# Blocks 12 to 15 of the first token group by Strassen's scheme too, its weight sums on GpSimd

## The chip, the cores and the metric

The kernel runs on one core of a Trainium2 chip. Such a core has a matrix engine (TensorE, PE in the profile; its weight loads are PEld), a vector engine (VectorE, DVE), an activation engine (ScalarE, ACT), a general one (GpSimd, POOL) and SyncE (SP), which here issues most DMAs. SBUF is the memory on the core with 128 partitions; PSUM holds the results of matmuls in banks. Each engine works through its own queue in order and waits on semaphores for the others.

The metric is the device time of one launch in microseconds (us). Times of several runs are given with their median; a profiled execution is one run more, of which a trace is kept.

## The reference

One layer of a streaming encoder for 2048 prompt tokens and 64 sample tokens: a modulated RMSNorm, one input projection, a pooling mixer beside an mLSTM, an output projection, then a second modulated RMSNorm and a gated MLP with a causal convolution of width 3. The change lies in the MLP:

```python
h2 = rmsnorm(x, g2) * (1 + sc2) + sh2
up = h2 @ w_up                                     # 1024 -> 2 * 2816
upp = jnp.concatenate([conv_buf.astype(up.dtype), up], 1)
conv = b_conv + sum(w_conv[j] * upp[:, j:j + T] for j in range(CONV_W))
a, g = jnp.split(conv, 2, -1)
x = x + gt2 * ((jax.nn.silu(g) * a) @ w_down)      # 2816 -> 1024
```

All is float32. The kernel gets that accuracy from a faster matmul by splitting each operand in a rounded part and a remainder and making three products of them (`PASSES`).

## The kernel before, in words

The MLP takes the 2112 tokens in three groups of 704 (`fgroups`, groups 0, 1 and 2, the loop `for o in fgroups`). The hidden width 2816 is 22 blocks of 128 (`f`). For each block, `Pair.products` makes the a and the g half of the up projection by a scheme of Strassen's kind: seven products (B11, T1, T2, B21, B22, T3 and, one block later, T4) of 12 matmuls with 352 columns each (L1604), which add into three PSUM banks, instead of eight. For the scheme, sums of the tokens' blocks are needed. They are made for the next group ahead of time by the generator `prepare`, one step at a time: it loads rows of x, scales them, makes seven sums for each of four row pairs, rounds each on ScalarE (L798), takes the remainder on DVE (L784) and further differences (L780), and stores both parts (`Bd`, L850, from ScalarE's queue). Its tiles come from four buffers named fscr.

The rest of a block is spread over the two blocks after it: sums and copies out of PSUM (`eg`, `ea`; L1613 on DVE, L1617 on ScalarE), the convolution (L1577 on ScalarE, two taps of eg and ea each on DVE, L1582), silu (L1801), the gate (L1806, or L1809 in a Strassen part) and the split of the result in two parts (`av`: L1884 on ScalarE and L1889 on DVE). The tiles ea and eg have one buffer each. Their first two columns come from a small buffer UC by a copy on GpSimd (L1560), and their last two go back there (L1574).

Blocks are put together in parts (`PARTS`). After the blocks of a part stands its down projection. A plain part runs `down`: for each of the eight output rows, per block, three matmuls of 448 and three of 256 columns (L2212). A part of four blocks can run `quad_down` instead: Strassen's scheme again, over two by two blocks, seven products in place of eight, 168 matmuls of 352 columns (L2073). Such a part is held: its operands (B11 to T4 of the class `Quad`, seven av tiles, made in `step_2` to `step_7`) are prepared while the next blocks start, and `quad_down` runs inside the first block of the next part. Group 1 does that for its blocks 0 to 19 (five quads), group 2 for 0 to 15 (four); group 0 does not, since `paired` asks for g > 0.

Weights come as a stream of units of 512 columns (`stream`, `issue`, `pump`), loaded up to seven ahead on SP's queue into raw or wt buffers. Each is rounded on ScalarE (L427) and its remainder taken on DVE (L430), some units ahead of use (`work_out`). For the down scheme four sums of weights for each pair of output rows are read from `dsum`, a buffer in DRAM. They are made once, in group 0, by the generator `quad_sums`: 20 halves, each one load (L1660), four tensor ops of 128x256 (L1664 to L1670) and one store (L1673), with pauses between.

What stands where is written by hand: from the MLP on, PE, ScalarE, DVE and GpSimd run in program order, and the order of SP's queue is the scheduler's. Side work is put in through lists (`bg`): `tick(i)` runs list i on to its next pause, `drain(i)` runs it to its end at once. `quad_sums` is in list 0, which gets two ticks in each product (14 a block) and some in `down`; `prepare` is in list 1, which gets four ticks a block and the other ticks of `down`. Where `todo` holds steps of the last blocks, `down` takes those instead of a tick. At the last part's down phase, lists 0 and 1 are drained, and list 1 gets the loads of the next group's operands.

## Time and profile before

| | us |
|---|---|
| median of three runs (2169.93 to 2173.72) | 2172.97 |
| the profiled execution, all in all | 2169.81 |
| its span, first instruction to last | 2168.0 |
| group 0 of the MLP, from its first up product on | 787.2 to 1251.6 |
| of it, its four down phases | 853.7, 959.6, 1078.1 and 1203.9, of 41 to 48 each |
| groups 1 and 2 | 1251.6 to the end |

A row of the profile that groups instructions has line, engine, operation, result<-operands, sizes, count, then busy time in us, mean ns of one, and the idle time of the engine before them with what ended it. A row of the timeline has its start in us, the time it covers, the instructions merged in it, and in square brackets idle time before it. A row of a stretch has its length, then the busy time of PE, PEld, DVE, ACT and POOL with counts in brackets, TensorE's granted clock, the DMA engines' busy share and GB/s. Numbers with L are lines of the kernel before; in the changed kernel the same lines stand one further down behind `SUMS`, and eight further behind the last hunk.

### The profile page before, as it was taken

Reading aid. Unit: us, or ns where it says so; the run is one execution under the profiler, and the core shown is the slowest. Engines: PE = TensorE matmul, PEld = TensorE weight load, DVE = VectorE, ACT = ScalarE, POOL = GpSimd, SP = SyncE. Lnnn points to the kernel's source line nnn. Section 1 sums busy time; section 2 is a strip of 40 time slices with the busy share of each in tenths; the row PEclk is TensorE's granted clock in tenths of the full one; section 3 lists DMA queues with packets and bytes.
Section 4 is the critical chain, followed back from the end, with each engine's and each line's share of the span. In section 5 each row is a group of like instructions: output and inputs, shape, how many; then the busy total and the mean of one; then the engine's idle time right before and its main releaser. Section 6 shows DMA issues by size and latency. Waiting matters only on the chain.

```text
span 2168.0 us, 38128 instructions
## 1 busy us (share of the span) xinstructions
PE 2146.5 (99%) x13529; PEld 2040.9 (94%) x13529; DVE 1666.4 (77%) x3107; ACT 1104.1 (51%) x2201; POOL 249.3 (12%) x468
## 2 busy tenths in 40 slices
PE   8999999999999999999999999999999999999998
PEld 7888888888899999999999999999999999999998
DVE  5777678677675878797968668988888797887874
ACT  4554335334333556464736445655656455565554
POOL 0010000001000301010101220100101121111112
PEclk9999999999999999999999999999999999999999
DMA  8987997897788686888968976666666875555542
GB/s 317 330 307 228 321 317 252 282 320 269 246 286 281 229 268 232 293 288 301 353 235 307 319 264 206 226 227 200 219 232 230 277 269 190 171 175 188 173 157 76
DMA packets 302439, 545.28 MB, mean 252 GB/s; under 512 B 25984, under 2 KB 118656, under 8 KB 302248
## 3 DMA queue, kind: packets, MB, share of 16 engines
q1 hardware_dynamic: 291656, 517.64, 70.6%
q10 hardware_dynamic: 10592, 25.20, 3.0%
q8 instruction: 107, 1.75, 0.3%
q14 instruction: 84, 0.69, 0.1%
HBM read 414.65 MB, written 128.08 MB: 250 GB/s over the span
## 4 chain that ended last, share of the span: by engine, by line
PE 60%; DVE 3%; DMA 1%; issue 1%; ACT 1%; POOL 0%; SPq 0%; DVEq 0%; POOLq 0%; ACTq 0%
PE mm L1604 37%; PE mm L2212 11%; PE mm L2073 10%; PE mm L494 2%; DVE wt L430 1%; DVE tg L1582 0%; ACT tg L1577 0%; DMA wt<-dsum 0%; DMA wt<-wsum 0%; DMA fscr<-h2d 0%; DVE ea L1613 0%; DVE eg L1613 0%; DVE x L2042 0%; DVE tg L1809 0%; ACT mm L1652 0%
## 5 line engine op out<-in xcount | busy, mean ns | idle before, releaser
L1604 PE MATMUL mm<-hx,wt 128*128 128x352 f32 x5544 | 887.1, 321 | 0.9 <-DVE wt L430 0.7
L1604 PEld LDWEIGHTS mm<-hx,wt 128*128 128x128 f32 x5544 | 880.5, 188 | 2.2 <-DVE wt L430 1.9
L494 PE MATMUL mm<-hl,wt 128*128 128x512 f32 (+2 forms) x1920 | 385.8, 356 | 0.3 <-DMA wt<-hl_kept 0.3
L427 ACT ACTIVATE wt<-raw 128x512 fp32r<-128x512 f32 (+3 forms) x468 | 275.9, 597 | 191.0 <-PE mm L494 53.4
L430 DVE TENSOR_TENSOR wt<-raw,wt 128x512 fp32r<-128x512 f32 (+3 forms) x468 | 307.3, 663 | 74.8 <-ACT wt L427 73.3
L494 PEld LDWEIGHTS mm<-hl,wt 128*128 128x128 f32 x1920 | 314.7, 188 | 48.1 <-issue 4.4
L2073 PE MATMUL mm<-av,wt 128*128 128x352 f32 x1512 | 248.2, 324 | 2.7 <-DVE ea L1613 1.2
L2073 PEld LDWEIGHTS mm<-av,wt 128*128 128x128 f32 x1512 | 242.3, 188 | 6.2 <-DVE ea L1613 4.0
L2042 DVE SCALAR_TENSOR_TENSOR x<-mm,MOD,x 128x352 f32<-128x352 f32 (+5 forms) x384 | 180.3, 508 | 69.0 <-PE mm L2212 54.1
L2212 PE MATMUL mm<-av,wt 128*128 128x448 f32 (+1 forms) x1440 | 232.2, 322 | 0.0
L2212 PEld LDWEIGHTS mm<-av,wt 128*128 128x128 f32 x1440 | 221.2, 188 | 9.9
L1652 ACT ACTIVATE mm<-mm 128x352 f32<-128x352 f32 x204 | 91.4, 448 | 235.9 <-PE mm L1604 176.6
L494 PE MATMUL mm<-mx,wt 128*128 128x512 f32 (+1 forms) x960 | 182.2, 351 | 1.2 <-DVE scr L266 1.2
L494 PEld LDWEIGHTS mm<-mx,wt 128*128 128x128 f32 x960 | 158.5, 188 | 24.1 <-DVE scr L266 1.1
L1582 DVE SCALAR_TENSOR_TENSOR ta<-ea,V,ta 128x704 f32<-128x704 f32 (+1 forms) x132 | 125.6, 952 | 54.8 <-ACT ta L1577 48.2
L1582 DVE SCALAR_TENSOR_TENSOR tg<-eg,V,tg 128x704 f32<-128x704 f32 (+1 forms) x132 | 125.7, 952 | 50.5 <-ACT tg L1577 48.0
L430 DVE TENSOR_TENSOR wt<-wt 128x512 fp32r<-128x512 f32 x204 | 138.4, 683 | 11.6 <-ACT wt L427 11.6
L427 ACT ACTIVATE wt<-wt 128x512 fp32r<-128x512 f32 x204 | 123.6, 622 | 34.0 <-DMA wt<-wsum 31.0
L1560 POOL COPY ea<-UC 128x2 f32<-128x2 f32 x66 | 32.7, 496 | 510.4 <-DVE ta L1582 429.1
L1801 ACT ACTIVATE tg<-tg 128x704 f32<-128x704 f32 (+1 forms) x66 | 52.4, 794 | 69.3 <-DVE tg L1582 69.3
L1143 PE MATMUL mm<-wt,hl 128*128 128x256 f32 (+1 forms) x576 | 71.2, 284 | 0.0
L1143 PEld LDWEIGHTS mm<-wt,hl 128*128 128x128 f32 x576 | 70.2, 189 | 0.8 <-issue 0.6
(306 smaller groups left out, 2220.2 us busy)
## 6 DMA issues: line engine op xcount, KB each, us to landing
wt<-wsplit SPq DMA_DIRECT2D x132, 512.0 KB, 4.3
raw<-w_up SPq DMA_DIRECT2D x198, 256.0 KB, 4.3
wt<-hl_kept SPq DMA_DIRECT2D x96, 512.0 KB, 6.3
wt<-wsum SPq DMA_DIRECT2D x132, 256.0 KB, 5.2
wsplit<-wt SPq DMA_DIRECT2D x66, 512.0 KB, 5.4
w<-w_up SPq DMA_DIRECT2D x88, 256.0 KB, 4.8
wsum<-w SPq DMA_DIRECT2D x44, 512.0 KB, 6.0
Bd<-fscr ACTq DMA_DIRECT2D x56, 352.0 KB, 4.4
```

The source lines that it names most:

```text
L427: act.activation(u.w[:, 0, :u.n], u.raw[:, :u.n], AF.Copy)
L430: dve.tensor_tensor(out=u.w[:, 1, :u.n], in0=u.raw[:, :u.n], in1=u.w[:, 0, :u.n].bitcast(F32), op=ALU.subtract)
L494: pe.matmul(ps[bi][:, :hi - lo], U[:, a, k % 4 * P:(k % 4 + 1) * P], mv[k][:, b, lo:hi], start=(at == 0 and pi == 0), stop=(k == order[-1] ...
L1143: pe.matmul(ps[ti][:n, :cols], h[4 * kh + k4][:, b, lo:lo + n], U[:, a, k4 % 2 * cols:(k4 % 2 + 1) * cols], start=(kh == 0 and k4 == 0 and ...
L1560: pool.tensor_copy(ext[:, 0:2], UC[:, f, :])
L1582: dve.scalar_tensor_tensor(out=t[:, :E], in0=ext[:, j:j + E], scalar=wc(j, f), in1=t[:, :E], op0=ALU.mult, op1=ALU.add)
L1604: pe.matmul(bk.t[:, :FH], U[:, a, kc * P:(kc + 1) * P], Bo.at(nm, kc, b), start=(first and kc == 0 and pi == 0), stop=(kc == 3 and pi == 2 ...
L1652: act.activation(to.t[:, :FH], bk.t[:, :FH], AF.Copy)
L1801: act.activation(self.tg[:, :E], self.tg[:, :E], AF.Silu)
L2042: dve.scalar_tensor_tensor(out=x3[n][:, a:b], in0=bk.t[:, a - lo:b - lo], scalar=gt2(n, s), in1=x3[n][:, a:b], op0=ALU.mult, op1=ALU.add)
L2073: pe.matmul(bk.t[:, :FH], U[:, a, c:c + P], quad.put(op, m, b), start=(first and m == 0 and pi == 0), stop=(m == 1 and pi == 2), skip_grou ...
L2212: pe.matmul(bks[i].t[:, :hi - lo], U[:, a, k % 4 * P:(k % 4 + 1) * P], av[k][:, b, lo:hi], start=(k == 0 and (a, b) == PASSES[0]), stop=(k ...
```

## The change

- Group 0's parts become (0, 6), (6, 12), (12, 16), (16, 22), and `paired` no longer asks for g > 0: blocks 12 to 15 of group 0 are a quad, held over into block 16.
- `quad_sums` takes a list of sums to make. The first list has twelve halves (6, 7, 0, 1, 2, 3; the first two are what the new quad reads), the second eight. The four ops of a half go to GpSimd, and a half takes eleven ticks in place of thirteen.
- Ahead of block 12 the first list is drained and list 1 (`prepare`) is put aside; behind `quad_down` it is put back, and the second list starts.
- At the last part's down phase of group 0 only list 1 is drained; list 0 at the end of that phase.

```diff
--- before.py
+++ after.py
@@ -30,13 +30,14 @@
 EB = 1
 AVB = 7
 ENDS = ((0, 448), (448, 704))
-PARTS = (((0, 5), (5, 10), (10, 16), (16, 22)), ((0, 4), (4, 8), (8, 12), (12, 16), (16, 20), (20, 22)),
+PARTS = (((0, 6), (6, 12), (12, 16), (16, 22)), ((0, 4), (4, 8), (8, 12), (12, 16), (16, 20), (20, 22)),
          ((0, 4), (4, 8), (8, 12), (12, 16), (16, 22)))
 NQ, QUADS = 4, 5
+SUMS = ((6, 7, 0, 1, 2, 3), (4, 5, 8, 9))
 
 
 def paired(g, part):
-    return g > 0 and part[1] - part[0] == NQ
+    return part[1] - part[0] == NQ
 EPS = 1e-6
 HD = 128
 NH = 4
@@ -1651,27 +1652,26 @@
 
         act.activation(to.t[:, :FH], bk.t[:, :FH], AF.Copy)
 
-    def quad_sums():
-
-        for d in range(2 * QUADS):
+    def quad_sums(ds):
+
+        for d in ds:
             for c in (0, 256):
                 t = f2.tile([P, 2, FT], F32R, tag="av", name="qs", bufs=AVB)
                 w = t.bitcast(F32).rearrange("p a t -> p (a t)")[:, :1024].rearrange("p (i c) -> p i c", i=4)
                 nc.sync.dma_start(out=w, in_=w_quad[d, :, :, c:c + 256])
-                for _ in range(5):
+                for _ in range(4):
                     yield
                 a11, a12, a21, a22 = (w[:, i] for i in range(4))
-                dve.tensor_tensor(out=a22, in0=a21, in1=a22, op=ALU.add)
-                yield
-                dve.tensor_tensor(out=a21, in0=a11, in1=a21, op=ALU.subtract)
-                yield
-                dve.tensor_tensor(out=a11, in0=a22, in1=a11, op=ALU.subtract)
-                yield
-                dve.tensor_tensor(out=a12, in0=a12, in1=a11, op=ALU.subtract)
+                pool.tensor_tensor(out=a22, in0=a21, in1=a22, op=ALU.add)
+                yield
+                pool.tensor_tensor(out=a21, in0=a11, in1=a21, op=ALU.subtract)
+                yield
+                pool.tensor_tensor(out=a11, in0=a22, in1=a11, op=ALU.subtract)
+                yield
+                pool.tensor_tensor(out=a12, in0=a12, in1=a11, op=ALU.subtract)
                 yield
                 yield
                 nc.sync.dma_start(out=dsum[d, :, :, c:c + 256], in_=w)
-                yield
                 yield
                 yield
 
@@ -2159,6 +2159,9 @@
             ends = o.last and lastp
             av = [None] * nf
             quad = Quad() if paired(o.g, part) else None
+            if quad is not None and o.g == 0:
+                drain(0)
+                aside, bg[1][:] = list(bg[1]), []
             if pi == 0:
                 pair = None
             for f in range(f0, f1_):
@@ -2169,16 +2172,19 @@
                 if held is not None and nf > 2:
                     quad_down(o, held, pair, old)
                     held = None
+                    if o.g == 0:
+                        bg[0].append(quad_sums(SUMS[1]))
+                        bg[1].extend(aside)
             if pi == 0 and o.g > 0:
                 drain(0)
                 x3 += load_x2(o, range(len(x3), KD))
             if not o.last:
                 if pi == 0:
                     if o.g == 0:
-                        bg[0].append(quad_sums())
+                        bg[0].append(quad_sums(SUMS[0]))
                     bg[1].append(prepare(fgroups[o.g + 1], fscr))
                 if lastp:
-                    drain(0, 1)
+                    drain(1) if o.g == 0 else drain(0, 1)
                     if nf == 2:
                         for p in (old, pair):
                             p.d = f1.tile([P, 2, HX], F32R, tag="hx", name="av", bufs=2 * len(BN))
@@ -2276,6 +2282,8 @@
             pair = None
         if not o.last:
             drain(1)
+            if o.g == 0:
+                drain(0)
             if nf == 2:
                 Bn = B[-1]
                 Bn.load(BN[-1])
```

How this moves instructions is shown at three places. ScalarE at the end of group 0, from the last copy of the up products (ea, L1617) to the last silu's followers. Before:

```order
L1617 ACTIVATE ea<-mm 128x352
L427 ACTIVATE wt<-raw 128x512
L1801 ACTIVATE tg<-tg 128x704
L427 ACTIVATE wt<-raw 128x512
L427 ACTIVATE wt<-raw 128x256 x2
L1884 ACTIVATE av<-tg 128x704
```

And in the changed kernel, with the stores of `prepare` (Bd) and its roundings (L799):

```order
L1801 ACTIVATE tg<-tg 128x704
L851 DMA Bd<-fscr 128x704
L799 ACTIVATE fscr<-fscr 128x352
L428 ACTIVATE wt<-raw 128x512
L851 DMA Bd<-fscr 128x704
L799 ACTIVATE fscr<-fscr 128x352
L851 DMA Bd<-fscr 128x704
L799 ACTIVATE fscr<-fscr 128x352
L851 DMA Bd<-fscr 128x704
L799 ACTIVATE fscr<-fscr 128x352
L851 DMA Bd<-fscr 128x704
L428 ACTIVATE wt<-raw 128x256 x2
```

Four roundings and five stores of `prepare` now stand between the silu and the splits of the first 256-column down units; before, none did.

DVE at the same place, from the last taps of g to the sum eg of block 21. Before:

```order
L1582 SCALAR_TENSOR_TENSOR tg<-eg,V,tg 128x704 x2
L430 TENSOR_TENSOR wt<-raw,wt 128x512 x3
L430 TENSOR_TENSOR wt<-raw,wt 128x256
L1613 TENSOR_TENSOR eg<-mm,s_13198 128x352
L1806 TENSOR_TENSOR tg<-ta,tg 128x704
```

In the changed kernel (L785 are remainders, L781 differences of `prepare`):

```order
L1583 SCALAR_TENSOR_TENSOR tg<-eg,V,tg 128x704 x2
L785 TENSOR_TENSOR fscr<-fscr 128x352
L781 TENSOR_TENSOR fscr<-fscr 128x352
L431 TENSOR_TENSOR wt<-raw,wt 128x512 x2
L785 TENSOR_TENSOR fscr<-fscr 128x352
L781 TENSOR_TENSOR fscr<-fscr 128x352 x2
L785 TENSOR_TENSOR fscr<-fscr 128x352 x3
L431 TENSOR_TENSOR wt<-raw,wt 128x512
L431 TENSOR_TENSOR wt<-raw,wt 128x256
L1614 TENSOR_TENSOR eg<-mm,s_13152 128x352
L1806 TENSOR_TENSOR tg<-ta,tg 128x704
```

Eight ops of `prepare` now stand ahead of eg, six of them without other work but the splits between.

GpSimd in blocks 8 and 9 of group 0, from the copy into ea of block 8 on. Before:

```order
L1560 COPY ea<-UC 128x2
L1560 COPY eg<-UC 128x2
L1574 COPY UC<-ea 128x2
L1574 COPY UC<-eg 128x2
L1560 COPY ea<-UC 128x2
```

In the changed kernel (L1665 to L1671 are the four ops of a half of the weight sums):

```order
L1561 COPY ea<-UC 128x2
L1665 TENSOR_TENSOR qs<-qs 128x256
L1667 TENSOR_TENSOR qs<-qs 128x256
L1669 TENSOR_TENSOR qs<-qs 128x256
L1561 COPY eg<-UC 128x2
L1671 TENSOR_TENSOR qs<-qs 128x256
L1575 COPY UC<-ea 128x2
L1575 COPY UC<-eg 128x2
L1561 COPY ea<-UC 128x2
```

Four ops on the weight sums now stand between the copies; before, GpSimd had the copies alone there, and the ops were DVE's.

## The prediction

> **What bounds the kernel now.** I read the page first (busy shares, chain, groups), then the timeline of TensorE for the stretch that the change touches, then DVE block by block, then the rows in which GpSimd and DVE meet.
>
> ```profile
> span 2168.0 us, 38128 instructions
> PE 2146.5 (99%) x13529; PEld 2040.9 (94%) x13529; DVE 1666.4 (77%) x3107; ACT 1104.1 (51%) x2201; POOL 249.3 (12%) x468
> PE 60%; DVE 3%; DMA 1%; issue 1%; ACT 1%; POOL 0%; SPq 0%; DVEq 0%; POOLq 0%; ACTq 0%
> L1604 PE MATMUL mm<-hx,wt 128*128 128x352 f32 x5544 | 887.1, 321 | 0.9 <-DVE wt L430 0.7
> ```
>
> TensorE is busy 99% of the span and leads the chain; the up products (L1604) idle 0.9 us in all. So only fewer matmuls can shorten the kernel, and any late operand lengthens it one for one. How near the operands are to late is read from the opening group by blocks. The next rows are stretches of one block each (blocks 12 to 15 with sums and preparation beside them, then 18 to 21 with sums in three of the four and no preparation): length, then busy time of PE, PEld, DVE, ACT and POOL with counts in brackets.
>
> ```profile
> 1024.88:1038.18 13.30, 13.30 (x87) 13.30 (x85) 12.60 (x22) 9.77 (x18) 2.58 (x4) 1.00 0.96 342
> 1038.18:1051.48 13.30, 13.30 (x87) 13.30 (x85) 12.44 (x21) 8.98 (x16) 2.75 (x4) 1.00 1.05 392
> 1051.48:1064.80 13.32, 13.32 (x87) 13.28 (x85) 13.18 (x22) 10.43 (x19) 2.56 (x4) 1.00 1.00 325
> 1064.80:1078.10 13.30, 13.30 (x87) 13.30 (x85) 12.82 (x23) 9.67 (x19) 2.13 (x4) 1.00 1.01 353
> ...
> 1150.67:1163.97 13.30, 13.30 (x86) 13.30 (x85) 12.10 (x20) 8.95 (x16) 2.29 (x4) 1.00 0.90 321
> 1163.97:1177.27 13.30, 13.30 (x87) 13.30 (x85) 12.01 (x20) 9.16 (x16) 2.30 (x4) 1.00 0.96 334
> 1177.27:1190.57 13.30, 13.30 (x87) 13.30 (x85) 12.01 (x20) 9.39 (x17) 2.30 (x4) 1.00 0.89 318
> 1190.57:1203.87 13.30, 13.30 (x86) 13.30 (x85) 10.66 (x16) 9.08 (x18) 2.29 (x4) 1.00 0.94 316
> ```
>
> With sums and preparation DVE fills 12.4 to 13.2 of 13.3 us: it keeps up with nothing to spare. Without either it takes 10.7; the sums are four instructions a block and some 1.4 us (12.0 less 10.7).
>
> **1. The down products of blocks 12 to 15: minus 3.4 us.** First a plain down phase of six blocks with the up product inside it, then one Strassen down phase of four blocks in group 1, last the group that holds all nine of them.
>
> ```profile
> 1203.87 4.04 PE L2212 MATMUL mm<-av,wt 128*128 128x448 f32 x24
> 1207.74 2.06 PE L1604 MATMUL mm<-hx,wt 128*128 128x352 f32 x12
> 1209.64 42.15 PE L2212 MATMUL mm<-av,wt 128*128 128x448 f32 x264
> ...
> 1399.37 4.19 PE L2073 MATMUL mm<-av,wt 128*128 128x352 f32 x24
> 1405.30 23.23 PE L2073 MATMUL mm<-av,wt 128*128 128x352 f32 x144
> ...
> L2073 PE MATMUL mm<-av,wt 128*128 128x352 f32 x1512 | 248.2, 324 | 2.7 <-DVE ea L1613 1.2 <-DVE x L2042 0.7 <-DVE wt L430 0.4
> ```
>
> Plain: 288 matmuls in 46.2 us, so the 192 of four blocks take 30.8. Strassen: 168 in 27.4. The difference is 3.4 us. The nine phases idle 2.7 us, 0.3 each, which I add (0 to 1.5, since waits fall unevenly and group 0 splits all seven weight units of a block where later groups reload three of them split). DVE gains per quad six weight splits, wider adds and the operand sums; in blocks 12 to 15 sums and preparation are away to make room, and I cost it at nothing more than that 0.3. Six blocks for five in the first two parts only move the boundary of plain phases whose rows show no gap: nothing.
>
> **2. The weight sums leave DVE for GpSimd: plus 5.5 us.** The rows: one of the four DVE lines that make the sums today, a GpSimd op of the same form, and a weight split on DVE; then how the two engines meet, in two places of the last plain down phase; last the busy times of a whole plain down phase.
>
> ```profile
> L1664 DVE TENSOR_TENSOR qs<-qs 128x256 f32<-128x256 f32 x20 | 8.4, 418 | 0.0
> L2022 POOL TENSOR_TENSOR y<-x,fscr 128x256 f32<-128x256 f32 x2 | 1.4, 723 | 1.8 <-ACT fscr L1990 1.8
> L430 DVE TENSOR_TENSOR wt<-wt 128x512 fp32r<-128x512 f32 x86 | 57.9, 685 | 10.6 <-ACT wt L427 10.6
> ...
> 1225.39 1.07 DVE L430 TENSOR_TENSOR wt<-raw,wt 128x512 fp32r<-128x512 f32 x1 [1.05 <-ACT wt L427]
> 1225.98 2.04 POOL L2034 TENSOR_TENSOR ssum<-ssum,fscr 128x704 f32<-128x704 f32 x1
> 1226.84 0.68 DVE L2042 SCALAR_TENSOR_TENSOR x<-mm,MOD,x 128x448 f32<-128x448 f32 x1 [0.38 <-PE mm L2212]
> ...
> 1230.40 1.70 POOL L2034 TENSOR_TENSOR ssum<-ssum,fscr 128x704 f32<-128x704 f32 x1 [2.38 <-ACT fscr L2033]
> 1230.82 1.84 DVE L430 TENSOR_TENSOR wt<-raw,wt 128x512 fp32r<-128x512 f32 x1 [1.05 <-ACT wt L427]
> ...
> 1078.10:1125.97 47.87, 47.87 (x303) 45.96 (x301) 32.11 (x60) 15.64 (x30) 1.28 (x4) 1.00 0.62 206
> ```
>
> A split that takes 0.685 us took 1.84 when it began inside a GpSimd add of 1.70 us: it ended 0.56 us after that add did. The GpSimd add of 1225.98 in turn took 2.04, because a split was under way. The L2042 op in the same add took its plain 0.68; it reads one operand from PSUM, the split reads both from SBUF. So a GpSimd add and a DVE op with two SBUF operands exclude each other. Nearly all of DVE's work in a block is of that kind (splits, taps, gates); the two L1613 sums are not.
>
> The price: from the end of the split at 1226.46 to the end of the GpSimd add at 1228.02 lie 1.56 us, and a next split would end 0.56 later: 2.12 us where DVE alone takes 0.685. A GpSimd add thus holds a full DVE queue for 1.43 of its 1.70 us, its own length less 0.27; for the 0.723 us form 0.45 us, or 0.72 where nothing of it is won back. DVE spends 0.42 on the same sum itself. So the move frees 80 x 0.42 = 33.6 us of DVE and locks it for up to 80 x 0.45 = 36 or more, unless the adds fall where DVE waits anyway. In the plain down phases they do (DVE busy 32 of 48 us above), and I cost those at nothing. In the blocks they don't. The recorded order has 28 adds between the ea copies of blocks 6 and 11, 21 of them from block 8 on; the older list gave 14 steps of 13 for four sums, some 17 in four blocks. Blocks 12 to 15 above are the like of the new 8 to 11: 51.0 us of DVE, less 17 x 0.42 = 43.9, plus 21 x 0.45 = 53.4 or 21 x 0.72 = 59.0, against 53.2 us of TensorE: 0.2 to 5.8 us late, and none if the adds meet L1613 and short waits. I take 3.5, above the middle, since adds stand in the queue four and five together and a gap once made on TensorE is not won back. Blocks 18 to 21 today take 46.8 us with twelve sums, so 41.8 without; preparation adds 2.9 (51.0 less four times 12.0), 17 adds 7.7 to 12.2: 52.4 to 56.9 against 53.2. I take 2.0 (0 to 3.7). That DVE is free of sums in other places gives nothing back: there is no wait to remove.
>
> [...]
>
> **3. Draining the first list ahead of block 12: plus 0.5 us (0 to 3).** Eight adds stand in a row before block 12's ea copy, and SP stores each sum behind them, with weight loads queued behind the store. Today's waits of SP for the sums are at most 2.5 us:
>
> ```profile
> SPq L1673 <- DVE qs L1670: 16.2, 12, 2.5
> ```
>
> Weights are loaded several us ahead at the end of a down phase, which hides one such wait.
>
> **4. The paused preparation ends in a heap: plus 8 us, and 2 for the clock.** Preparation has 91 steps. It is now driven in fewer places, and the recorded order shows what is left when the last part's products are out: on ScalarE, right behind the last silu, five stores of operand sums (Bd) with four roundings between them and no other work but one split; on DVE the four remainders of the same chain (L784) and two subtractions (L780) ahead of the eg sum of block 21. All four fscr buffers are in use, two of them by the rows, so a rounding waits until the store two before it has landed. The rows: five such stores in today's trace (the first, second and last) with two of the waits, the landing time, then the place where the heap now stands.
>
> ```profile
> 1091.63 0.33 ACTq L850 DMA_DIRECT2D Bd<-fscr  x1
> 1094.35 0.33 ACTq L850 DMA_DIRECT2D Bd<-fscr  x1
> 1096.46 0.50 ACT L798 ACTIVATE fscr<-fscr 128x352 fp32r<-128x352 f32 x1 [1.70 <-DMA Bd<-fscr]
> ...
> 1098.80 0.50 ACT L798 ACTIVATE fscr<-fscr 128x352 fp32r<-128x352 f32 x1 [1.84 <-DMA Bd<-fscr]
> ...
> 1102.59 0.33 ACTq L850 DMA_DIRECT2D Bd<-fscr  x1
> ...
> DMA to landing us min/median/max: 2.2/4.4/6.9
> ...
> 1202.34 0.79 ACT L1801 ACTIVATE tg<-tg 128x704 f32<-128x704 f32 x1 [0.69 <-DVE tg L1582]
> ...
> 1204.63 0.52 DVE L1613 TENSOR_TENSOR eg<-mm,s 128x352 f32<-128x352 f32 x1
> ```
>
> Five stores took 11.0 us, first to last. Behind the silu, which ends at 1203.1, the last is issued at 1214.1; a 256-wide split on ScalarE and on DVE (0.42 each) and eg (0.52) follow: 1215.5. TensorE's T4 product adds into the bank that eg reads, and begins at 1207.74. It is 7.8 us late; I take 8. Were the landings free, four roundings and four subtractions of 0.5 in turn make 4 us and the wait 1.3; with DVE two us behind from term 2 it is 10. Range 0 to 10.
>
> So long a gap on TensorE may cost clock too: its first matmuls, after idling, against four of the same form right behind other matmuls, and the last 8 us of the span, where TensorE is nearly idle and the granted clock (the third number from the end) is 0.58 on average.
>
> ```profile
> 5.44 6.41 PE L1042 MATMUL m<-mx 128*128 128x256 f32 x16 [5.44 <-DMA mx<-xT]
> 17.37 1.03 PE L1061 MATMUL m<-mx 128*128 128x256 f32 x4
> ...
> 2160.00:2168.00 8.00, 1.16 (x8) 0.97 (x8) 2.54 (x7) 0.38 (x1) 1.60 (x3) 0.58 0.69 252
> ```
>
> 0.40 us each against 0.26: 16 lost 2.3 us. I add 2 (0 to 3.2, half of that 6.41 us stretch). [...]
>
> **Sum.** -3.4 + 0.3 + 5.5 + 0.5 + 8 + 2 = +12.9 us. The profiled execution took 2169.81 us in all (span 2168.0), at the lower edge of the three runs (2169.93 to 2173.72, median 2172.97). Against the median: 2186.
>
> **The rivals.** (a) Not slower: the heap is hidden. The preparation's last steps would have to end before T4 wants its bank. For it: stores can land in 2.2 us, and down phases forgive much elsewhere. Against it: eg stands behind all of it in DVE's order and has 2.6 us to spare today. Without terms for heap and clock the sum is +2.9, 2176; the heap decides from a wait of 1.4 us on (4.3 us, 0.2% and about what a measurement can tell here, less 2.9). (b) GpSimd's lock dominates: the adds are not spread as the steps are but run as soon as their data are there, four or five in a row, against blocks whose weights are ready just in time. Each of ten blocks then stalls up to five adds' worth less a us of lead: some 15 us where I took 5.5, 2195. For it: DVE's fill above. Against it: a GpSimd add lets a DVE op in between. (c) SP: twenty stores of sums wait for a GpSimd that itself waits, and the weight loads behind them come late, a us each: plus 20, 2206. Against it: SP waits only 16.2 us in all for these stores now, and TensorE feels none of it. (d) It just works: no lock, no heap, -3.1 us, 2170.
>
> **How the numbers follow.** Forecast (2180 to 2191) 0.54; (a) 0.12; (b) 0.20; (c) 0.10; (d) 0.04. Slower takes the forecast, (b), (c); (a) lies half within 0.2%, half above; (d) falls within, with a little below by the spread of runs. Slower 0.87, same 0.10, faster 0.03. The range 2176 to 2198 leaves out (d), part of (a), (c).
>
> **What would show it.** L2073 with 1680 matmuls and L2212 with 1248; the sums' lines on POOL with means above 0.72 us, and L430's mean in blocks 6 to 11 and 17 to 21 well above 0.685 us with TensorE gaps ended by it; a gap of some 8 us ahead of block 21's T4 product, ended by DVE's eg, and slow clock behind it. Wrong if the gap is under 2 us or L430 keeps its mean.

## The result, and the profile after

The changed kernel takes 2195.46 us (median of five runs, 2192.05 to 2198.33) against 2172.71 of the kernel before beside it (2169.93 to 2173.72): a ratio of 1.0106, 95% interval 1.0091 to 1.0122, some 23 us slower. The forecast was 2186, 13 us slower. The profiled execution took 2192.05 us. From the page of the changed kernel:

```profile
span 2190.3 us, 38100 instructions
PE 2152.7 (98%) x13505; PEld 2042.9 (93%) x13505; DVE 1674.0 (76%) x3047; ACT 1112.8 (51%) x2213; POOL 331.4 (15%) x548
PE 53%; DVE 4%; DMA 4%; issue 2%; ACT 1%; POOL 1%; SPq 0%; DVEq 0%; ACTq 0%; POOLq 0%
L1605 PE MATMUL mm<-hx,wt 128*128 128x352 f32 x5544 | 894.0, 322 | 16.2 <-DVE wt L431 6.4
L2073 PE MATMUL mm<-av,wt 128*128 128x352 f32 x1680 | 275.5, 323 | 1.7 <-DVE x L2042 0.7
L2218 PE MATMUL mm<-av,wt 128*128 128x448 f32 (+1 forms) x1248 | 202.9, 324 | 1.8 <-DVE wt L431 1.8
```

Lines ahead of the sums are numbered one higher (the splits are L428 and L431, the up products L1605), L2042 and L2073 keep their numbers, and the plain down, L2212, is L2218. The work moved as written: 1680 and 1248 matmuls. The up products, which idled 0.9 us before, now idle 16.2, and DMA's share of the chain is 4% instead of 1%. Where, says TensorE's timeline of the same kernel, in blocks 9 to 11, then in the new Strassen down, then in blocks 20 and 21:

```profile
970.23 5.97 PE L1605 MATMUL mm<-hx,wt 128*128 128x352 f32 x26 [1.91 <-ACT mm L1653]
977.11 13.58 PE L1605 MATMUL mm<-hx,wt 128*128 128x352 f32 x84 [0.92 <-DVE wt L431]
992.13 9.67 PE L1605 MATMUL mm<-hx,wt 128*128 128x352 f32 x58 [1.44 <-DVE wt L431]
...
1119.27 4.20 PE L2073 MATMUL mm<-av,wt 128*128 128x352 f32 x24
1123.30 2.06 PE L1605 MATMUL mm<-hx,wt 128*128 128x352 f32 x12
1125.20 23.21 PE L2073 MATMUL mm<-av,wt 128*128 128x352 f32 x144
...
1204.43 13.26 PE L1605 MATMUL mm<-hx,wt 128*128 128x352 f32 x82 [1.58 <-DVE wt L431]
1219.87 5.25 PE L2218 MATMUL mm<-av,wt 128*128 128x448 f32 x22 [1.78 <-DVE wt L431]
1230.96 3.64 PE L1605 MATMUL mm<-hx,wt 128*128 128x352 f32 x12 [5.84 <-DVE eg L1614]
```

The table gives stretches of group 0 in the profiled executions, each from the first up product of a block to the first of another, so a down phase lies in the block in which it starts. Without gaps, blocks 6 to 11 would take 126.6 us (five of 13.3, and 60.1 for one with a six-block down phase, as block 5 has it), blocks 17 to 20 53.2 and block 21 59.2, as before. The ratios are taken against runs of the kernel before on the same chip (4 to 10 runs of the one, 5 to 21 of the other). Since its median there lay between 2170.7 and 2173.1, kernels are compared by the third column, the part of the ratio above 1 times 2172.7 us; its intervals are 3 to 4 us to either side (2 for e4 and c1).

| kernel | median, us | ratio to before (interval) | over before, us | 6 to 11 | 17 to 20 | 21 | group 0 |
|---|---|---|---|---|---|---|---|
| before | 2172.7 | | 0 | | 53.2 | 59.2 | 464.4 |
| after | 2195.5 | 1.0106 (1.0091–1.0122) | 23.0 | 137.5 | 57.9 | 70.3 | 487.3 |
| e1, sums on DVE | 2188.2 | 1.0070 (1.0055–1.0085) | 15.2 | 131.3 | 61.6 | 68.5 | 483.6 |
| e2, no pause | 2193.5 | 1.0090 (1.0073–1.0107) | 19.6 | 137.6 | 54.1 | 65.9 | 486.8 |
| e2b, no heap | 2190.5 | 1.0092 (1.0077–1.0107) | 20.0 | 141.3 | 57.1 | 61.0 | 481.1 |
| e3b, sums on DVE, no heap | 2181.7 | 1.0051 (1.0036–1.0066) | 11.1 | 129.9 | 60.1 | 59.2 | 471.9 |
| e5, no sums | 2179.2 | 1.0042 (1.0027–1.0057) | 9.1 | 128.9 | 53.4 | 68.8 | 473.3 |
| e6, one operand | 2196.9 | 1.0112 (1.0093–1.0131) | 24.3 | 138.7 | 58.0 | 72.5 | 490.9 |
| e7, late store | 2187.7 | 1.0069 (1.0052–1.0086) | 15.0 | 134.7 | 56.6 | 69.0 | 482.4 |
| e8, held store | 2195.6 | 1.0113 (1.0096–1.0130) | 24.6 | 135.4 | 57.2 | 70.0 | 484.2 |
| x, lock alone | 2191.2 | 1.0083 (1.0068–1.0098) | 18.0 | 134.0 | 57.3 | 69.6 | 486.8 |
| e4, before with sums on GpSimd | 2178.0 | 1.0023 (1.0014–1.0033) | 5.0 | | 53.2 | 59.4 | 471.3 |
| c1, early sums | 2176.1 | 1.0019 (1.0009–1.0028) | 4.1 | 129.8 | 59.3 | 59.2 | 472.2 |
| c2, early preparation | 2180.9 | 1.0034 (1.0020–1.0049) | 7.4 | 129.7 | 55.9 | 59.7 | 475.8 |

After against before, group 0 is 22.9 us longer: 10.9 in blocks 6 to 11, 4.7 in blocks 17 to 20, 11.1 at block 21, and 3.8 less elsewhere, about what the Strassen down saves (30.8 less 27.1). One profile of a stretch is not exact: blocks 6 to 11 run the same instructions in after, e2 and e2b and took 137.5 to 141.3.

Three readings come before the experiments. First the heap, from the timelines of ScalarE and DVE of the changed kernel:

```profile
1218.15 0.33 ACTq L851 DMA_DIRECT2D Bd<-fscr  x1
...
1225.73 0.50 ACT L799 ACTIVATE fscr<-fscr 128x352 fp32r<-128x352 f32 x1 [3.97 <-DMA Bd<-fscr]
...
1229.13 0.33 ACTq L851 DMA_DIRECT2D Bd<-fscr  x1
...
1230.30 0.52 DVE L1614 TENSOR_TENSOR eg<-mm,s 128x352 f32<-128x352 f32 x1
```

Five stores in 11.0 us, and eg, which TensorE's T4 waits for, behind them. Second, blocks 9 and 10. From the timelines of SP and ScalarE, then SP's waits at this store in blocks 6 to 10 (total, times, longest):

```profile
954.63 1.50 SPq L407 DMA_DIRECT2D raw<-w_up  x2
962.55 0.52 SPq L1674 DMA_DIRECT2D dsum<-qs  x1
963.17 1.56 SPq L415 DMA_DIRECT2D wt<-wsum  x2
...
968.29 0.63 ACT L428 ACTIVATE wt<-wt 128x512 fp32r<-128x512 f32 x1 [2.28 <-DMA wt<-wsum]
...
SPq L1674 <- POOL qs L1671: 12.4, 3, 5.2
...
SPq L1674 <- POOL eg L1561: 6.0, 1, 6.0
```

SP stood 6.4 us at the store of a sum, since GpSimd had not made it (both rows of waits name GpSimd; it began 1.3 us into that time, when the load had landed). The weight loads behind that store went out at 963.17, ScalarE waited for one of them, and the gap of 1.91 us that ends at 970.23 follows: the chain of rival (c). Third, DVE and GpSimd in blocks 6 to 10 of the same kernel (busy us, mean ns):

```profile
L431 DVE TENSOR_TENSOR wt<-wt 128x512 fp32r<-128x512 f32 x19 | 13.8, 742 | 7.4 <-ACT wt L428 7.4
L431 DVE TENSOR_TENSOR wt<-raw,wt 128x512 fp32r<-128x512 f32 x15 | 12.5, 835 | 0.4 <-ACT wt L428 0.4
...
L1667 POOL TENSOR_TENSOR qs<-qs 128x256 f32<-128x256 f32 x5 | 5.4, 1081 | 0.3
L1665 POOL TENSOR_TENSOR qs<-qs 128x256 f32<-128x256 f32 x5 | 5.3, 1067 | 14.6 <-DMA qs<-w_quad 14.6
```

Splits take 0.74 and 0.84 us instead of 0.685, GpSimd's twenty adds 0.98 on average instead of 0.72 (1.07 and 1.08 in the two lines shown): the lock of rival (b) is there too. Which of the two costs the time the profile alone doesn't say.

### The profile page after: what moved, and what is told of

The parts are those of the page before. It is cut to its first block, busy times and chain, and to the rows that moved or that the text cites. A ratio compares the mean times of both kernels' runs of the same rounds, so it can differ in the third digit from the quotient of the medians.

```text
span 2190.3 us, 38100 instructions
## 1 busy us (share of the span) xinstructions
PE 2152.7 (98%) x13505; PEld 2042.9 (93%) x13505; DVE 1674.0 (76%) x3047; ACT 1112.8 (51%) x2213; POOL 331.4 (15%) x548
## 4 chain that ended last, share of the span: by engine, by line
PE 53%; DVE 4%; DMA 4%; issue 2%; ACT 1%; POOL 1%; SPq 0%; DVEq 0%; ACTq 0%; POOLq 0%
PE mm L1605 32%; PE mm L2073 11%; PE mm L2218 9%; PE mm L495 2%; DVE wt L431 1%; DMA wt<-wsum 1%; DMA wsplit<-wt 1%; DVE tg L1583 1%; DMA qs<-w_quad 1%; ACT tg L1578 0%; DMA wt<-dsum 0%; DMA Bd<-fscr 0%; DMA fscr<-h2d 0%; DVE ta L1583 0%; DVE eg L1614 0%
## 5 line engine op out<-in xcount | busy, mean ns | idle before, releaser
L1605 PE MATMUL mm<-hx,wt 128*128 128x352 f32 x5544 | 894.0, 322 | 16.2 <-DVE wt L431 6.4
L1605 PEld LDWEIGHTS mm<-hx,wt 128*128 128x128 f32 x5544 | 883.0, 188 | 22.1 <-DVE wt L431 10.4
L431 DVE TENSOR_TENSOR wt<-raw,wt 128x512 fp32r<-128x512 f32 (+2 forms) x458 | 312.7, 689 | 77.9 <-ACT wt L428 77.6
L428 ACT ACTIVATE wt<-raw 128x512 fp32r<-128x512 f32 (+2 forms) x458 | 273.8, 604 | 177.4 <-PE mm L495 54.7
L2073 PE MATMUL mm<-av,wt 128*128 128x352 f32 x1680 | 275.5, 323 | 1.7 <-DVE x L2042 0.7
L2073 PEld LDWEIGHTS mm<-av,wt 128*128 128x128 f32 x1680 | 269.3, 188 | 5.1 <-DVE ea L1614 3.1
L2042 DVE SCALAR_TENSOR_TENSOR x<-mm,MOD,x 128x352 f32<-128x352 f32 (+4 forms) x392 | 184.0, 510 | 55.9 <-PE mm L2218 39.2
L2218 PE MATMUL mm<-av,wt 128*128 128x448 f32 (+1 forms) x1248 | 202.9, 324 | 1.8 <-DVE wt L431 1.8
L2218 PEld LDWEIGHTS mm<-av,wt 128*128 128x128 f32 x1248 | 192.9, 189 | 10.7 <-DVE wt L431 2.2
L431 DVE TENSOR_TENSOR wt<-wt 128x512 fp32r<-128x512 f32 x212 | 146.0, 696 | 18.8 <-ACT wt L428 18.7
L428 ACT ACTIVATE wt<-wt 128x512 fp32r<-128x512 f32 x212 | 128.5, 622 | 42.3 <-DMA wt<-wsum 38.9
L1144 PEld LDWEIGHTS mm<-wt,hl 128*128 128x128 f32 x576 | 70.3, 189 | 0.8 <-issue 0.6
```

Source lines behind the costliest of these rows:

```text
L428: act.activation(u.w[:, 0, :u.n], u.raw[:, :u.n], AF.Copy)
L431: dve.tensor_tensor(out=u.w[:, 1, :u.n], in0=u.raw[:, :u.n], in1=u.w[:, 0, :u.n].bitcast(F32), op=ALU.subtract)
L1144: pe.matmul(ps[ti][:n, :cols], h[4 * kh + k4][:, b, lo:lo + n], U[:, a, k4 % 2 * cols:(k4 % 2 + 1) * cols], start=(kh == 0 and k4 == 0 and ...
L1605: pe.matmul(bk.t[:, :FH], U[:, a, kc * P:(kc + 1) * P], Bo.at(nm, kc, b), start=(first and kc == 0 and pi == 0), stop=(kc == 3 and pi == 2 ...
L2042: dve.scalar_tensor_tensor(out=x3[n][:, a:b], in0=bk.t[:, a - lo:b - lo], scalar=gt2(n, s), in1=x3[n][:, a:b], op0=ALU.mult, op1=ALU.add)
L2073: pe.matmul(bk.t[:, :FH], U[:, a, c:c + P], quad.put(op, m, b), start=(first and m == 0 and pi == 0), stop=(m == 1 and pi == 2), skip_grou ...
```

## The experiments

Edits are against the changed kernel unless another is named.

**The sums on VectorE again (e1).**

```diff
-                pool.tensor_tensor(out=a22, in0=a21, in1=a22, op=ALU.add)
+                dve.tensor_tensor(out=a22, in0=a21, in1=a22, op=ALU.add)
```

and the same in the other three lines of the sums.

> The four operations of the weight sums are on VectorE again, as before the change; lists, pause and the Strassen down of blocks 12 to 15 stay as after the change. Theory GpSimd (its sums cost blocks 6-11 11.8 us and blocks 17-21 4.5 us in the traces, whether through VectorE's slower splits or through SyncE's queue): the two stretches fall back to about 78 and 65 us and the heap of 11 us at the end of the opening group stays, so about 2195.5 - 14 = 2181 (2178 to 2185). Rival two-lists (the shorter stretches into which the sums are pressed cost the time, whichever engine does them): no less than 2191, with VectorE's sums of 0.42 us each in the way instead.

Measured: 2188.2, between the two theories. GpSimd in VectorE's place costs 7.8 us here (23.0 less 15.2). But with the sums on VectorE blocks 6 to 11 are still 4.7 us over and blocks 17 to 20 8.4, more than with GpSimd. TensorE's timeline of e1:

```profile
987.93 13.87 PE L1605 MATMUL mm<-hx,wt 128*128 128x352 f32 x82 [2.07 <-DVE wt L431]
...
1202.01 14.57 PE L1605 MATMUL mm<-hx,wt 128*128 128x352 f32 x82 [3.16 <-DVE wt L431]
```

So the stretches into which the sums are now put have no room for them on either engine.

**GpSimd's move alone, in the kernel before (e4).** The same four lines changed the other way, in the kernel before.

> The kernel before with one edit, the four operations of the sums on GpSimd: one list of 13 steps per half, no Strassen down in the opening group, no pause. Theory GpSimd (its sums cost wherever they stand): 80 additions lock about 0.45 us each as in the prediction, most of it in stretches where VectorE has room: 5 to 10 us slower than before, 2177 to 2182. Rival pace (they cost only where 12 halves are pressed into six blocks at 11 steps): 2170 to 2174.

Measured: 2178.0, ratio 1.0023: 5 us slower, the lower end of what the first theory gave. The move costs with the old pace too, if less.

**One operand instead of two on GpSimd (e6).**

```diff
-                pool.tensor_tensor(out=a22, in0=a21, in1=a22, op=ALU.add)
+                pool.tensor_scalar(out=a22, in0=a21, scalar1=0.5, scalar2=None, op0=ALU.mult)
```

> GpSimd's four operations per half now read one tile and multiply it by a constant instead of adding two tiles: as many instructions of the same size on the same engine, in the same places, with the same loads and stores; the sums themselves are left out, so the down-projection of blocks 0 to 11 uses wrong weights. Theory lock (an operation with two operands in SBUF on GpSimd stretches the splits of weights on VectorE): the splits in blocks 6-11 return to about 0.69 us, the stretches to 80 and 66 us: about 2182 (2179 to 2186). Theory queue (SyncE's store of the sums waits for GpSimd, and the loads of weights behind it are late): GpSimd is as late as before, the time stays at 2191 to 2196.

(Here and in the two runs that follow all the sums are left out, so the weights are wrong in every Strassen down phase that reads them.) Measured: 2196.9, as after. In blocks 6 to 10 the splits are nearly free again, and SP waits longer than after the change. First the splits of e6 on DVE, then its SP waits (total, times, longest), the store with the longest, and its gap:

```profile
L431 DVE TENSOR_TENSOR wt<-wt 128x512 fp32r<-128x512 f32 x20 | 14.1, 710 | 14.5 <-ACT wt L428 13.6 <-DMA qs<-w_quad 0.8
...
SPq L1674 <- POOL eg L1561: 9.9, 2, 5.6
SPq L1674 <- POOL UC L1575: 7.3, 1, 7.3
...
956.61 1.65 SPq L407 DMA_DIRECT2D raw<-w_up  x2
966.88 0.52 SPq L1674 DMA_DIRECT2D dsum<-qs  x1
...
973.18 0.63 ACT L428 ACTIVATE wt<-wt 128x512 fp32r<-128x512 f32 x1 [7.18 <-DMA wt<-wsum]
...
975.12 15.01 PE L1605 MATMUL mm<-hx,wt 128*128 128x352 f32 x84 [5.89 <-ACT mm L1653]
```

ScalarE waits 7.18 us for a weight that SP issued late, and TensorE stands 5.89. So late sums are enough with VectorE nearly free of the lock. But the lateness is not that of the changed kernel: SP stood 8.6 us at the store shown where it had stood 6.4.

**No sums (e5).** The four operations are taken out; loads and stores stay.

> The four operations of the sums are left out, their loads and stores stay where they are: the down-projection of blocks 0 to 11 uses wrong weights. Theory queue: the store waits for the landing of its load only, so SyncE's waits shrink but don't go; blocks 6-11 fall from 137.5 to about 130, the heap stays: about 2186 (2182 to 2189). Rival crowding: the transfers are all there, 2191 to 2196. If GpSimd's operations matter only by their work, it would be as the sums on VectorE without VectorE's own part, 2184 to 2187.

Measured: 2179.2, the bound of 2182 passed by 3 us. Blocks 17 to 20 are free (53.4) and blocks 6 to 11 2.3 us over; what is left is the heap, 9.6 us at block 21. The transfers crowd nothing: the rival falls. It is the four operations that cost 13.9 us (23.0 less 9.1), on VectorE 6.1 (15.2 less 9.1). In blocks 6 to 10 of e5, split and longest SP wait for this store:

```profile
L431 DVE TENSOR_TENSOR wt<-wt 128x512 fp32r<-128x512 f32 x19 | 12.7, 687 | 5.7 <-ACT wt L428 5.7
...
SPq L1670 <- DMA qs<-w_quad: 13.0, 3, 4.4
```

SP still waits 13.0 us there, for the landing of the load, 4.4 at most, and TensorE feels little of it; after the change SP waited 18.4 us for GpSimd and 3.3 for the load, up to 6.0. So, as an estimate from these two runs, the weights loaded ahead cover about 4 us, and GpSimd's slow sums push the wait past that.

**The lock alone (x).** No sums as in e5, and in their places adds of the same size on a tile that nothing else uses:

```diff
-                pool.tensor_tensor(out=a22, in0=a21, in1=a22, op=ALU.add)
+                pool.tensor_tensor(out=zz[:, :256], in0=zz[:, 256:], in1=zz[:, :256], op=ALU.add)
```

> The sums are left out (the down-projection of blocks 0 to 11 uses wrong weights); in their places GpSimd adds two halves of a tile of its own, of the same size, which nothing waits for; loads and stores of the sums stay. So GpSimd's two operands in SBUF are there, and its lateness is not: nobody waits for it. Without any operation there it was 2179. Theory lock alone is enough: VectorE's splits are at about 0.78 us again and the time is 2187 to 2195. Theory lateness (the lock costs only where the store of the sums waits too): 2179 to 2183.

Measured: 2191.2, as the first theory had it, and 8.9 us above e5 by the ratios. No engine waits for these adds, SP stands for the load of this store about as long as in e5 in blocks 6 to 10 (12.7 us, 13.0 there), and still blocks 6 to 11 take 134.0 (128.9 in e5), blocks 17 to 20 57.3 (53.4), and block 5 with its down phase 4.1 us more. One such place, from the timelines of GpSimd, DVE and TensorE of x, then a group of DVE in blocks 6 to 10, last the gap in the down phase of block 11:

```profile
972.79 1.27 POOL L1670 TENSOR_TENSOR zz<-zz 128x256 f32<-128x256 f32 x1
...
972.27 2.54 DVE L1583 SCALAR_TENSOR_TENSOR tg<-eg,V,tg 128x704 f32<-128x704 f32 x2 [0.15 <-ACT tg L1578]
974.74 1.05 DVE L785 TENSOR_TENSOR fscr<-fscr 128x352 fp32r<-128x352 f32 x1
975.82 0.93 DVE L781 TENSOR_TENSOR fscr<-fscr 128x352 f32<-128x352 f32 x1
976.68 0.68 DVE L431 TENSOR_TENSOR wt<-raw,wt 128x512 fp32r<-128x512 f32 x1
...
977.41 13.57 PE L1605 MATMUL mm<-hx,wt 128*128 128x352 f32 x84 [1.65 <-DVE wt L431]
...
L1583 DVE SCALAR_TENSOR_TENSOR tg<-eg,V,tg 128x704 f32<-128x704 f32 x8 | 9.0, 1122 | 3.1 <-ACT tg L1578 3.0
...
1024.87 33.12 PE L2221 MATMUL mm<-av,wt 128*128 128x448 f32 x197 [2.05 <-DVE av L1892]
```

Two taps of 0.95 us take 2.54, an L785 of 0.52 takes 1.05; the split that TensorE waits for comes late by about what TensorE stands. The splits themselves take 0.71 us on average in x, not the 0.78 expected and no more than in e6; it is the taps and the remainders that are longer. In all, VectorE's operations in blocks 6 to 10 took 4.5 us more in x than at their durations in e5, 1.6 in e6 and some 6 after the change.

By this and e6, lock and lateness can each cost time without the other, and they don't add up: over e5 x costs 8.9 us, e6 15.2 (24.3 less 9.1), the changed kernel with both 13.9. What each costs in the changed kernel is not shown, since x does not lose its time in the same places. Blocks 17 to 20 are alike (57.3, 58.0 in e6, 57.9 after the change). But blocks 6 to 10 take 69.4 us in x, 67.6 in e5, 77.4 in e6 and 76.7 after the change: there the lock alone costs 1.8 us of 9.1. The rest of x's loss lies in the down phases of blocks 5 and 11, 4.1 and 3.3 us over e5, where the changed kernel loses nothing against e5; perhaps the adds, with no load to wait for, run close together there, which is not shown.

**The store of the sums later (e7, e8).** In e7 it is issued five steps after the last sum instead of two, the load stands a step closer to the sums, and a half takes twelve steps instead of eleven:

```diff
-                for _ in range(4):
+                for _ in range(3):
                     yield
...
                 yield
                 yield
+                yield
+                yield
+                yield
                 nc.sync.dma_start(out=dsum[d, :, :, c:c + 256], in_=w)
                 yield
-                yield
```

> GpSimd keeps the sums as after the change, but the store of each half's sums is issued four steps later (some 6 us), so that SyncE finds the sums done; the load stands one step later too. Theory queue: blocks 6-11 lose the gaps of 1.9 and 1.4 us and most of the 11.8 us, about 2183 (2180 to 2187). Theory lock: splits stay at about 0.9 us or more beside the sums and the time stays at 2192 to 2196.

In e8 it is kept until just ahead of the next half's sums:

```diff
+                while held:
+                    nc.sync.dma_start(**held.pop())
                 a11, a12, a21, a22 = (w[:, i] for i in range(4))
...
-                nc.sync.dma_start(out=dsum[d, :, :, c:c + 256], in_=w)
+                held.append(dict(out=dsum[d, :, :, c:c + 256], in_=w))
```

> The sums stay on GpSimd, but the store of each half's sums is held back until just ahead of the next half's sums, six steps later than after the change; everything else as after. Theory queue (SyncE stands 5.5 to 6.4 us at each store for GpSimd, and the weight loads behind it are late): SyncE's wait at this store falls below 4 us in all in blocks 6-11, their time from 137.5 to about 129, blocks 17-21 lose 2: about 2195.5 - 10 = 2185.5 (2182 to 2188). Rival crowding (the loads and stores of the sums take the transfers that the weights need, whenever they are issued): 2191 to 2196.

Measured: 2187.7 and 2195.6. By the ratios e7 gains 8.0 us, between its two theories, and e8 nothing. In the traces blocks 6 to 11 gain 2.8 and 2.1 us, not the 8 that SyncE's queue was to be worth by itself, and no more than such stretches vary. SP's waits at this store in blocks 6 to 10 did fall, to 13.7 and 13.1 us with 5.0 and 4.5 the longest, about as in e5, though not below the 4 us that e8's theory named. The adds still meet DVE (in e7 the medians of the four lines on GpSimd are 0.74, 0.82, 0.93 and 0.98 us, the shortest add 0.72), which fits the loss that is left but doesn't prove it. In e7 blocks 17 to 21 gain 2.6 too; as its slower pace puts 16 sums instead of 20 into blocks 6 to 10, its gain is not the late store's alone. In e8 a new wait takes back what group 0 won (3.1 us), at its end. From the timelines of GpSimd and TensorE of e8:

```profile
1273.27 0.74 POOL L1668 TENSOR_TENSOR qs<-qs 128x256 f32<-128x256 f32 x1 [12.98 <-DMA qs<-w_quad]
1273.96 1.72 POOL L2039 TENSOR_TENSOR ssum<-ssum,fscr 128x704 f32<-128x704 f32 x1
...
1281.90 1.48 PE L1929 MATMUL m<-ones_r,ssum 128*128 128x1 f32 x12 [2.90 <-POOL ssum L2039]
```

The last half's load comes late behind the held store; GpSimd stands 12.98 us for it, with the sum of squares of the final norm behind in its program order, and block 22 takes 20.3 us instead of 15.4. The expected 2185.5 was missed by 10 us.

**No pause (e2).** `aside` is left out, so the preparation goes on through blocks 12 to 15 and their down phase.

> The preparation is no longer set aside ahead of block 12: it goes on through blocks 12 to 15 and their down-projection; the sums stay on GpSimd in two lists. Theory heap (five stores of operands and four roundings behind one another, 11.0 us, hold back block 21's last operand T4; +11.1 us in the traces): the gap of 5.84 us ahead of block 21's T4 and the slow clock around it go, about 2195.5 - 11 = 2184.5 (2182 to 2188). Rival work (the preparation takes the same time from VectorE and ScalarE wherever it lies): the Strassen down of blocks 12 to 15 becomes as much longer, 2192 or more.

Measured: 2193.5, 3.4 us better than after where 11 were expected. The heap is gone, and the preparation costs elsewhere, as the rival had it: blocks 12 to 15 take 55.4 instead of 53.3 and block 16 with the Strassen down 45.2 instead of 40.4; block 21 keeps 6.7 us over its 59.2. From TensorE's timeline of e2, in the Strassen down and in block 21:

```profile
1129.99 1.75 PE L2073 MATMUL mm<-av,wt 128*128 128x352 f32 x6 [2.35 <-DVE ea L1614]
...
1222.62 5.64 PE L1605 MATMUL mm<-hx,wt 128*128 128x352 f32 x24 [2.07 <-ACT mm L1653]
```

**The rest of the preparation step by step (e2b, e3b).** The pause stays, the heap goes:

```diff
-                    drain(1) if o.g == 0 else drain(0, 1)
+                    if o.g > 0:
+                        drain(0, 1)
```

> The preparation stays paused as after the change, but what is left of it at block 21 is not run off in one heap: it goes on step by step in the down-projection of blocks 16 to 21, and the reloads of group 1's operands follow it. Theory heap (what costs is that the rest stands in one place ahead of block 21's T4): the gap of 5.8 us and the slow clock around it go, about 2195.5 - 10 = 2185.5 (2183 to 2188). Rival work (the rest of the preparation and the later reloads cost the same wherever they stand): the down-projection or the first blocks of group 1 become longer, 2191 to 2196.

Measured: 2190.5, 3.0 us better than after. Blocks 17 to 21 fall by 10.0 us, as expected of the heap, but the reloads of group 1's operands now come behind the preparation and block 22 takes 18.3 instead of 15.4:

```profile
1274.87 0.75 PE L1605 MATMUL mm<-hx,wt 128*128 128x352 f32 x3 [1.64 <-DMA hx<-Bd]
```

The other 3.8 us lie in blocks 6 to 11, in front of the edit, whose instructions are the same: what a profile of the same stretch varies by. With the sums on VectorE as well (e3b):

> The sums on VectorE again and the rest of the preparation step by step as in the run without the heap; lists, pause and the Strassen down of blocks 12 to 15 stay. If the two parts add up: 2188.2 for the sums on VectorE less 10 for the heap, about 2178 (2175 to 2181), still slower than before, since blocks 6-11 were 4.7 us above their matmuls with the sums on VectorE. If the costs are one and the same (late weights and late operands for which the preparation or the sums are each enough): 2185 or more. If the Strassen down's 3.4 us are all that is left: 2169 to 2171.

Measured: 2181.7, 11.9 us better than after; e1 alone gave 7.8 and e2b alone 3.0, so the two parts add up within what the runs can tell. The 2178 expected (up to 2181) counted the heap at 10 us and was missed; over e1 its removal gives 4.1.

**A version that keeps the Strassen down (c1, c2).** c1 is e3b with the first list longer and started at block 0:

```diff
-SUMS = ((6, 7, 0, 1, 2, 3), (4, 5, 8, 9))
+SUMS = ((6, 7, 0, 1, 2, 3, 4, 5), (8, 9))
...
             if pi == 0:
                 pair = None
+                if o.g == 0:
+                    bg[0].append(quad_sums(SUMS[0]))
```

and twelve steps per half.

> The Strassen down of blocks 12 to 15 stays. Sums on VectorE; the first list holds 16 halves of 12 steps and starts with block 0, so that it has 12 blocks instead of 6, the second holds 4 halves; the rest of the preparation goes on step by step (no heap). Theory pace (the sums and the preparation cost time because they are pressed together): of 2181.7 of the same without the early start, the 3.3 us of blocks 6-11 and most of 6.9 us of blocks 17-21 go: 2172 to 2176. Full gain of the Strassen down: 2167 to 2170. If the Strassen down itself costs its neighbours this, with or without the pace: 2180 or more.

Measured: 2176.1, the edge of what pace gave; 0.19% slower than before and 0.9% faster than after. But the trace doesn't bear pace out: blocks 6 to 11 and group 0 are as in e3b, and the 4.7 us between the two spans lie mostly outside group 0. In c2 the preparation is set aside only ahead of the Strassen down itself:

> As the early sums, and the preparation also goes on through the products of blocks 12 to 15 and is set aside for the Strassen down alone, so that less of it is left for blocks 16 to 21. Theory pace: a further 1 to 3 us off blocks 17-21, 2169 to 2174. Rival work (the preparation costs blocks 12-15 what it spares later, as it did in the run without the pause): the same as with the early sums alone.

Measured: 2180.9. Blocks 17 to 20 gain 3.4 us, and blocks 12 to 16 lose 6.9 (55.4 and 45.2 again): as in e2. No version here beats the kernel before.

## Why the prediction was right or wrong

- **Direction, range, heap: right.** The time lies in the stated range, above the forecast's own 2180 to 2191. The heap was there, five stores in 11.0 us as worked out from five like stores of before, and the gap ahead of T4 is 5.84 us, shorter than the 8 forecast, with the clock at 0.50 around it (3.41 us from 1220.54 on, 6.83 from 1227.36 on) and a gap of 1.78 just before. The 2 us for the clock were an estimate from the span's first matmuls; here the 22 matmuls from 1219.87 on took 5.25 us, where as many of this form took 3.70 in e6 (from 1224.81 on), and the 12 of T4 3.64 us, where 12 take 2.06 at 1123.30. Block 21 takes 11.1 us more (9.6 in e5, without the sums); 8 and 2 were forecast. e2b, which takes the heap away, gets 10.0 back in blocks 17 to 21. In the run's time it gets 3.0: of the rest the late reloads explain 2.9 and blocks 6 to 11, ahead of the edit, 3.8.
- **The Strassen down: right.** 168 matmuls in 27.1 us (the timeline above, less the up product inside it) for a forecast of 27.4; group L2073 idles 1.7 us, not more than before. The drain ahead of block 12 (0.5): block 11 took 60.8 in place of 60.1.
- **Term 2, the sums: wrong in size.** 5.5 us forecast; blocks 6 to 11 and 17 to 20 took 10.9 and 4.7 more, 15.6. This 10 us is the whole miss. e5 bears the size out: without the four operations 13.9 us are gone. The term failed at two steps. The price of an add on a full DVE queue (0.45) wasn't one of them: x's place above lost DVE about 1.6 us by four adds, and in blocks 6 to 10 of the changed kernel twenty adds lost it some 6. The first is that the blocks were reckoned to have room for the sums, as long as DVE's own busy time stayed under TensorE's. e1 shows that on VectorE, too, the sums cost 6.1 us in these lists (15.2 less 9.1). Its blocks 6 to 10 hold 24 sums and 59.2 us of DVE's work and lose 4.7 us; blocks 10 to 14 of the kernel before held 22 and 58.6 and lost nothing. So DVE's busy time didn't tell whether there was room. The second is that SP's wait for GpSimd's sums was left to rival (c) at a price of its own, and today's waits of at most 2.5 us were taken for a bound. SP then stood up to 6.4 us.
- **The rivals.** The time is that of (b), 2195, which is in part luck: x shows that its mechanism costs time by itself, but only 1.8 us in blocks 6 to 10. In e6 the mechanism of (c) costs as much as both, with DVE nearly free. (c) was priced at 2206 because each of twenty stores was thought to cost, where by e5 a wait of some 4 us costs little. Anyone who had added (b) to (c) would have been wrong as well: in blocks 17 to 20 x, e6 and the changed kernel lose the same. (a) and (d) fall.
- **"L430 is well above 0.685 with gaps ended by it"** held in the letter (0.74 and 0.84, gaps of 0.92, 1.44 and 1.58 us ended by it), but e1 shows that such a row doesn't name the cause: its splits take 0.685 us, and its gaps of 2.07 and 3.16 us are ended by them just the same.

Open is why blocks 9 and 10 lose 3 to 4 us and blocks 17 to 20 some 6 with the sums on VectorE at a slower pace (c1), where before the change the same sums and the preparation left no gap. The trace of e1 has one hint: DVE's work lies unevenly there, 7.1 us in block 6 and 15.3 in block 10, where in blocks 10 to 14 of the kernel before no block had more than 13.2. But a block that is held up also takes in work of the next, so cause and effect are not told apart; no run varied that alone.

## What to carry to other kernels

Work moved to an idle engine wasn't free here, its result being stored from a queue that carries the critical loads (in e6 SP stood 8.6 us and TensorE 5.89): count how long such a queue can stand still (here, by estimate, about 4 us) and compare it with load, landing and work in a row. Before side work is pressed into fewer blocks, work out block by block how late it may come without harm, not the busy share; here four blocks at 96% busy lost nothing before the change, and five with 59.2 us of work in 66.5 did in e1. Where two causes cover each other, an experiment that removes one and changes nothing does not acquit it; and one that leaves only one says what that cause can cost, in the places where it then falls.

## What the runs showed of the hardware

**Behind gaps of 1.78 us and more the clock was 0.50.** Windows of 3.41 us of the changed kernel, the last but one of two such lengths (length, PE busy with its count, granted clock, DMA share, GB/s):

```profile
967.95:971.36 3.41, 1.50 (x10) 1.00 1.00 361
971.36:974.78 3.42, 3.42 (x14) 0.50 1.02 387
988.42:991.83 3.41, 2.27 (x15) 1.00 1.05 400
991.83:995.25 3.42, 3.12 (x19) 1.00 0.94 342
1203.47:1206.88 3.41, 2.45 (x15) 1.00 1.03 400
1206.88:1210.30 3.42, 3.42 (x24) 1.00 0.75 207
1217.13:1220.54 3.41, 1.63 (x11) 1.00 0.70 276
1220.54:1223.95 3.41, 3.41 (x14) 0.50 1.03 336
1223.95:1227.36 3.41, 1.17 (x8) 1.00 0.99 308
1227.36:1234.19 6.83, 3.23 (x11) 0.50 1.06 395
1234.19:1237.60 3.41, 3.41 (x22) 1.00 1.07 387
```

A gap of 1.91 us, or of 1.78, in one window is followed by a whole window at half clock, and so are the 2.24 us that TensorE idles between 1223.95 and 1227.36; one of 1.58, of which 0.96 falls in the window shown, is not. The half-clock stretches of the changed kernel start on one grid of 3.41 us: at 971.36, 1220.54, 1227.36 and, near its end, 2183.10. In its middle the windows of this grid that idled 1.78 us or more stand ahead of half clock; those ahead of full clock idled 1.14 at most (988.42 to 991.83). That is one execution, and gives no limit. What half a clock costs, the matmuls say: the 26 from 970.23 on took 5.97 us, 26 of the same form in e6 4.38 (from 990.41 on), 1.6 less. That makes the gap of 1.91 us cost 3.5, not one for one as the prediction had it; behind the one of 1.58, 82 matmuls took 13.26 us at full clock.

**The lock, for the most part.** The prediction left open whether DVE loses 0.45 or 0.72 us to an add. In x, from the start of the four adds at 971.52 to 976.68, GpSimd did 2.9 us of work by its plain durations (four of 0.72) and DVE some 3.4: 6.3 us of work in 5.2, so for the most part they exclude each other there. With one input on GpSimd (e6) DVE lost 1.6 us in blocks 6 to 10 instead of some 6.
